# A third seven-product pair in the odd gate/up blocks, with two of its weight sums moved to idle rows

## The chip, the core and the metric

The kernel runs on one core of a Trainium2 chip, the other cores idle. The metric is the device time of one execution in microseconds (us); lower is better. Each execution is one launch that reads all weights from HBM once and writes the output. Five engines work at the same time, each through its own queue in order: PE (TensorE, the matmuls), DVE (VectorE), ACT (ScalarE), POOL (GpSimd, which only issues small DMAs in the part that matters here) and SP (SyncE, which issues the weight loads).

## The reference

One decoder layer on 256 tokens of width 2048: a gated feed-forward network, a mixer (linear attention and dilated attention side by side), and a second gated feed-forward network. The change touches the first half of the two feed-forward networks alone:

```python
D_MODEL, SEQ, D_FF = 2048, 256, 5632

def swiglu(x, w_gate, w_up, w_down):
    return (jax.nn.silu(x @ w_gate) * (x @ w_up)) @ w_down

x = x + 0.5 * swiglu(rms_norm(x, ffn1_norm), ffn1_w_gate, ffn1_w_up, ffn1_w_down)
... # mixer
x = x + 0.5 * swiglu(rms_norm(x, ffn2_norm), ffn2_w_gate, ffn2_w_up, ffn2_w_down)
```

Everything is float32. The matmuls run in a reduced form (fp32r), so each operand is cut into a high part and a low rest, and a product is made of three matmuls: high by high, high by low, low by high.

## The kernel before, in words

**Gate/up.** `x @ w_gate` and `x @ w_up` are computed together in 11 blocks of 512 columns (`FF // 512`), in each feed-forward network. A block has 16 slices of the inner dimension of 128 rows each, taken as 8 k-pairs. One load on SP's queue (L220) brings a k-pair's weights, 1 MB, into the tile `raw`, laid out [128, 2 slices, gate and up, 512]; there are three `raw` buffers. The tokens are two groups of 128, so a block's result is four PSUM banks of 128x512: two token groups times gate and up.

**A plain k-pair.** Each of its two slices is a unit. `split` cuts the 128x1024 weights of a unit: ACT copies them to the high part `wh` (L114), then DVE subtracts to get the rest `wl` (L115). `products` (L277, L279, L281) then issues 12 matmuls for the unit: two token groups, two banks, three each. A plain k-pair costs 24 matmuls, 2 copies on ACT and 2 subtractions on DVE.

**A seven.** In the blocks of `FF_SEVEN` (1 to 10) two of the eight k-pairs are computed as a 2x2 by 2x2 block product with seven block products in place of eight (Winograd's form of Strassen's method). `seven_products` issues 21 matmuls (L302 to L304). For that, `seven` prepares the weights in four parts, in this order:

- `plain`: a 128x1024 sum into `room["sum"]` (DVE, L241), and the split of two of the raw quarters;
- `last`: the split of the fourth quarter alone, 128x512, into tiles of its own (`swh`, `swl` in the profile);
- `sums`: two 128x512 additions in place in `raw` (L249, the second needs the first), and the split of `room["sum"]`;
- `more`: the split of the two quarters of `raw` that hold those additions.

The sums of activations that a seven needs (`seven_forms`, L320 to L326 and a split) are made once for each feed-forward network and used by all of its blocks. k-pairs 0 and 1 are the sevens of every block, so there are two such sets, `forms[0]` and `forms[1]`.

**The fold and the evacuation.** The seven products accumulate partly in the four banks of the result (`cs`), partly in four others (`ms`). After the last seven of a block, `fold` combines the four `ms` banks: one ACT copy (L483) and four DVE additions (L484 to L487), one for each step, into the four rows p1, u1, u2, u3 of `xs[:, 1, :]`. At the end of the block `evac` adds those rows to the banks, applies silu and the product (L451 to L454), transposes in 32x32 squares (L129), has POOL issue 16 small DMAs for each token group (L136), and a later step `finish` splits the result into `uh`, `ul`. Between a block's evacuation and the next block's fold the four rows are idle.

**The order.** `FF_ORDERS` writes the order of plain (s) and seven (g) k-pairs in a block: `ssgssgss` in blocks 1 to 10, `ssssssss` in block 0. `weights()` keeps the prepared weights up to three units ahead of the matmuls, but the order on each engine is set when the program is built, by a scheduler that estimates times; an instruction can be placed ahead of earlier lines if its inputs are ready. What limits how far DVE and ACT run ahead of PE are the buffers: four each of `wh` and `wl`, one `swh`, `swl`, one `room["sum"]`, three of `raw`. Side jobs (`later`: the `finish` steps, in block 1 also `seven_forms`) are spread over the steps of the plain units of a block, two steps a unit.

**The rest.** The down projections and the output projection have sevens too, through the same function `seven`, with `rooms["down"]`.

Of the kernel before, what the change touches and what calls it, by code (L numbers as in the profile page):

```python
# [28 lines left out]
EPS = 1e-6  # L29
WBUF = 4  # L30
FF_SEVEN = range(1, 11)
TAIL = 4
WARM = 10
GH, GDK, GDV, RANK = 4, 128, 256, 16
# [7 lines left out]
    return [(next(seven), True) if c == "g" else (next(plain), False) for c in text]  # L42


FF_ORDERS = [_order("ssgssgss" if b in FF_SEVEN else "ssssssss") for b in range(FF // 512)]
DOWN_ORDERS = [_order("ssssssgssgssgsgsgsgsss"), _order("sgsssgssgssgssgsgsssss")]
OUT_ORDERS = [_order("ssssssss"), _order("ssgsgsss")]

# [1 line left out]
def layer_kernel(tc, x, xT, gains, gla_gate_up, gla_gate_bias, gla_out_norm, att_q_norm, att_k_norm,  # L50
# [6 lines left out]
    with ExitStack() as es:  # L57
# [135 lines left out]
        def wtile(name):  # L193
            return wp.tile([P, 2, 512], F32R, name=name, tag=name, bufs=WBUF)
# [39 lines left out]
        def seven(part, w):  # L234

            raw = raws[0].bitcast(F32)
            room = rooms["gate" if w is w_ff1 or w is w_ff2 else "down"]
            if part == "plain":
                b1 = raw[:, 0, 0, :].unsqueeze(1).to_broadcast([P, 2, 512])
                mid = raw.rearrange("p k j f -> p (k j) f")[:, 1:3, :]  # L240
                nc.vector.tensor_add(room["sum"], b1, mid)  # L241
                wh, wl = wtile("wh"), wtile("wl")
                split(wh, wl, mid)
            elif part == "last":
                wh, wl = room["wh"], room["wl"]
                split(wh[:, 0, :], wl[:, 0, :], raw[:, 1, 1, :])
            elif part == "sums":
                for j, b in enumerate((room["sum"][:, 0, :], raw[:, 1, 0, :])):
                    nc.vector.tensor_add(raw[:, 1, j, :], b, raw[:, 1, j, :])  # L249
                wh, wl = wtile("wh"), wtile("wl")  # L250
                split(wh, wl, room["sum"])
            else:
                wh, wl = wtile("wh"), wtile("wl")
                split(wh, wl, raw[:, 1])
            ready.append((wh, wl))

        def weights(early=False):
# [173 lines left out]
        def ffn(name, done, residual, extra=None, final=False):  # L431

            with tc.tile_pool(name=name, bufs=1, reuse_waits="tile") as fp:

                tail = FT - TAIL
                us_h = [fp.tile([P, tail, S], F32R, name="uh")]
                us_l = [fp.tile([P, tail, S], F32R, name="ul")]
                spare = ExitStack()
                urs = xs[:, 0, 0:NT * 512].rearrange("p (t f) -> p t f", t=NT)
                extra_sums, tails = [], []  # L440

                def part(k):
                    n = int(k >= tail)
                    return us_h[n], us_l[n], k - n * tail

                for b in range(FF // 512):
                    def evac(t, ps, b=b):
                        sg, u = t512("sg"), t512("u")
                        if b in FF_SEVEN:
                            rest = extra_sums[2 * t:2 * t + 2]  # L450
                            nc.vector.tensor_sub(halves(sg), ps[0], rest[0])  # L451
                            nc.scalar.activation(sg, sg, AF.Silu, scale=rt[:, t:t + 1])
                            nc.vector.tensor_add(rest[1], ps[1], rest[1])
                            nc.vector.scalar_tensor_tensor(halves(u), rest[1], rt[:, t:t + 1], halves(sg), op0=ALU.mult, op1=ALU.mult)  # L454
                        else:
                            nc.scalar.activation(halves(sg), ps[0], AF.Silu, scale=rt[:, t:t + 1])
                            nc.vector.scalar_tensor_tensor(halves(u), ps[1], rt[:, t:t + 1], halves(sg), op0=ALU.mult, op1=ALU.mult)

                        us = t512("us")
                        ur = urs[:, t, :]  # L460
                        squares(us, u)
                        move_squares(ur, us)

                        def finish():
                            uh, ul, k = part(4 * b)
                            split(*(runs(a[:, k:k + 4, t * P:(t + 1) * P]) for a in (uh, ul)), in_order(ur))

                        put = later if 4 * b < tail else tails
                        put.extend([lambda: None] * (2 if t else 6) + [finish])
                    if b == FF_SEVEN[0]:  # L470
                        sp = spare.enter_context(tc.tile_pool(name=name + "s", bufs=1, reuse_waits="tile"))
                        t4 = xs[:, 1, :].rearrange("p (i f) -> p i f", i=4)
                        p1, u1, u2, u3 = [halves(t4[:, i, :]) for i in range(4)]
                        extra_sums = [u1, p1, u3, u2]
                        room = rooms["gate"] = {"sum": xs[:, 0, NT * 512:].rearrange("p (j f) -> p j f", j=2)}
                        for n in ("wh", "wl"):
                            room[n] = sp.tile([P, 1, 512], F32R, name="s" + n)
                        fs = [sp.tile([P, 2, 4, P], F32R, name="f" + n) for n in "hl"]
                        forms = {kp: [f[:, kp] for f in fs] for kp in range(2)}
                        later[:0] = [lambda kp=kp: seven_forms(hacts[2 * kp:2 * kp + 2], forms[kp], t4[:, 0, :], t4[:, 1, :]) for kp in range(2)]  # L480

                        def fold(m):
                            return [lambda: nc.scalar.activation(p1, m[0], AF.Copy),  # L483
                                    lambda: nc.vector.tensor_add(u1, p1, m[2]),  # L484
                                    lambda: nc.vector.tensor_add(u2, u1, m[3]),
                                    lambda: nc.vector.tensor_add(u1, u1, m[1]),
                                    lambda: nc.vector.tensor_add(u3, u2, m[1])]  # L487
                    if b in FF_SEVEN:
                        seven_pair(hacts, FF_ORDERS[b], forms, b % 2, evac, fold)
                    elif b:  # L490
                        column_pair(hacts, evac)
                    else:
                        column_pair(hacts, evac, span=16, due=8 if final else 15, extra=extra)
                spare.close()
                nc.gpsimd.dma_start(xs[:, 1, :], residual[P:2 * P, :])
                rp = spare.enter_context(tc.tile_pool(name=name + "t", bufs=1, reuse_waits="tile"))
                us_h.append(rp.tile([P, TAIL, S], F32R, name="uh2"))
                us_l.append(rp.tile([P, TAIL, S], F32R, name="ul2"))
                urs = rp.tile([P, NT, 512], F32, name="urs")
                later.extend(tails + [lambda: nc.gpsimd.dma_start(xs[:, 0, :], residual[0:P, :])])  # L500

                dacts = [part(k) for k in range(FT)]

                rooms["down"] = {"sum": urs, "wh": lent(hl, 8, 0), "wl": lent(hl, 10, 0)}
                dforms = {kp + 1: [lent(hh, 2 * kp, 1), lent(hl, 2 * kp, 1)] for kp in range(4)}
                dforms[0] = [lent(hh, 12, 1), lent(hh, 14, 1)]
                dforms[5] = [lent(hl, 12, 1), lent(hl, 14, 1)]
                rest, later[:] = later[:], []
                for step in range(32):
                    kp = step // 5 - 1  # L510
                    if step % 5 == 0 and 0 <= kp < 6:
                        later.append(lambda kp=kp: seven_forms(dacts[2 * kp:2 * kp + 2], dforms[kp], t512("full"), t512("sums")))
                    else:
                        later.append(rest.pop(0) if rest else lambda: None)
                for cp in range(2):
                    def evac(t, ps, cp=cp):
                        for j in range(2):
                            c = 2 * cp + j
                            blk = xs[:, t, c * 512:(c + 1) * 512]
                            nc.vector.scalar_tensor_tensor(halves(blk), ps[j], 0.5, halves(blk), op0=ALU.mult, op1=ALU.add)  # L520
                            done(t, c, blk)

                    def fold(m, cp=cp):
                        return fold_into_xs(m, cp, urs, 0.5)

                    holding[0] = NT - cp
                    seven_pair(dacts, DOWN_ORDERS[cp], dforms, cp, evac, fold, span=28 if cp else 32, final=final and cp == 1)
                spare.close()
# [459 lines left out]
```

## Time and profile before

| | us |
|---|---|
| median of three runs | 1718.4 |
| lowest, highest | 1717.45, 1718.85 |
| span of the profiled execution, first to last instruction | 1715.9 |
| PE busy in it | 1705.4 |
| DVE busy | 1416.9 |
| ACT busy | 947.1 |

The span leaves out what lies before the first and after the last instruction; the median of the runs stands 2.5 us above it. Lines of the profile name an engine, a line of the kernel, an operation and its tiles (`wl<-raw,wh`), how often it ran, and the idle time before it with what ended it (`[0.43 <-DMA raw]`). In a timeline the first number is the start in us from the beginning of the span, the second the duration. In the first feed-forward network, gate/up block 3 runs on PE from 130.94 us to 171.10 us, blocks 1 and 2 before it and block 4 after it in steps of the same length.

### The profile page before, as it was taken

To read this page: it belongs to the slowest core of one execution; us is meant where nothing else is said; L and a number is where in the kernel's file an instruction comes from. 1 tells how busy PE (TensorE), PEld (TensorE's weight loads), DVE (VectorE), ACT (ScalarE), POOL (GpSimd) and SP (SyncE) were. 2 spreads that over 40 slices of the span, in tenths; PEclk is the share of its full clock that TensorE was granted. 3 is DMA by queue.
4 is the path that set the end of the run, shared out by engine and by line. 5 is a ranking of instruction groups with operands and counts; after the bars stand their busy time and mean duration, and the time that the engine had idled before them with its cause. 6 is when DMAs were issued, how large, how long until landed. Compare 5 with 4: busy or idle time off the path is not lost.

```text
span 1715.9 us, 22309 instructions
## 1 busy us (share of the span) xinstructions
PE 1705.4 (99%) x7974; PEld 1485.1 (87%) x7974; DVE 1416.9 (83%) x1731; ACT 947.1 (55%) x1173; POOL 505.7 (29%) x1002
## 2 busy tenths in 40 slices
PE   9999999999999999999999999999999999999999
PEld 7888888888888888888888888888888888888887
DVE  6888889898898788577865788788888898898876
ACT  7555555555555555564654555555555555555453
POOL 0333334344410611054250043333333333420000
PEclk9999999999999999999999999999999999999999
DMA  8666666556665657577564467666666666665654
GB/s 345 213 229 224 219 211 232 208 213 236 234 250 219 217 203 244 192 237 235 195 210 172 148 198 269 210 231 225 222 224 220 226 212 224 218 242 222 248 204 147
DMA packets 85807, 378.62 MB, mean 221 GB/s; under 512 B 21392, under 2 KB 38800, under 8 KB 42688
## 3 DMA queue, kind: packets, MB, share of 16 engines
q1 hardware_dynamic: 50864, 350.25, 57.2%
q0 software_dynamic: 34112, 25.88, 5.3%
q8 instruction: 62, 1.02, 0.2%
q10 hardware_dynamic: 720, 1.07, 0.2%
q14 instruction: 49, 0.40, 0.1%
HBM read 354.57 MB, written 4.19 MB: 209 GB/s over the span
## 4 chain that ended last, share of the span: by engine, by line
PE 89%; DMA 4%; DVE 4%; POOL 1%; issue 1%; ACT 0%; DVEq 0%; SPq 0%; ACTq 0%; POOLq 0%
PE acc L279 20%; PE acc L277 20%; PE acc L281 20%; PE tp L281 4%; PE tp L277 4%; PE tp L279 4%; PE acc L303 4%; PE acc L304 4%; PE acc L302 4%; DVE wl L115 2%; DMA raw<-in_w_dn_dram 2%; DMA hh<-us 1%; PE tp L303 1%; PE tp L304 1%; PE tp L302 1%
## 5 line engine op out<-in xcount | busy, mean ns | idle before, releaser
L114 ACT ACTIVATE wh<-raw 128x1024 fp32r<-128x1024 f32 (+1 forms) x660 | 683.6, 1048 | 531.2 <-PE acc L281 186.6
L115 DVE TENSOR_TENSOR wl<-raw,wh 128x1024 fp32r<-128x1024 f32 (+1 forms) x658 | 790.3, 1215 | 168.4 <-ACT wh L114 165.0
L136 POOL DMA_DIRECT2D xs<-us x704 | 344.9, 497 | 552.1 <-ACT wh L114 200.3
L281 PE MATMUL acc<-wh,hl 128*128 128x512 f32 x1232 | 370.7, 380 | 0.0
L279 PE MATMUL acc<-wl,hh 128*128 128x512 f32 x1232 | 369.9, 380 | 0.1
L277 PE MATMUL acc<-wh,hh 128*128 128x512 f32 x1232 | 363.5, 381 | 2.6 <-ACT wh L114 2.6
L277 PEld LDWEIGHTS acc<-wh,hh 128*128 128x128 f32 x1232 | 232.3, 189 | 37.7 <-ACT wh L114 4.1
L279 PEld LDWEIGHTS acc<-wl,hh 128*128 128x128 f32 x1232 | 232.6, 189 | 33.9 <-issue 0.7
L281 PEld LDWEIGHTS acc<-wh,hl 128*128 128x128 f32 x1232 | 232.6, 189 | 32.9 <-DVE hl L544 0.2
L279 PE MATMUL acc<-wl,uh 128*128 128x512 f32 x384 | 117.2, 380 | 0.0
L281 PE MATMUL acc<-wh,ul 128*128 128x512 f32 x384 | 117.0, 379 | 0.0
L277 PE MATMUL acc<-wh,uh 128*128 128x512 f32 x384 | 112.1, 380 | 0.7 <-ACT wh L114 0.7
L136 POOL DMA_DIRECT2D hh<-us x128 | 62.4, 506 | 126.7 <-DVE us L129 69.0
L241 DVE TENSOR_TENSOR xs<-raw 128x1024 f32<-128x1024 f32 x40 | 49.0, 1225 | 46.9 <-DMA raw<-in_w_ff_dram 46.9
L277 PEld LDWEIGHTS acc<-wh,uh 128*128 128x128 f32 x384 | 72.3, 189 | 12.0 <-ACT wh L114 1.9
L279 PEld LDWEIGHTS acc<-wl,uh 128*128 128x128 f32 x384 | 72.4, 189 | 10.8 <-DVE wl L115 0.6
L281 PEld LDWEIGHTS acc<-wh,ul 128*128 128x128 f32 x384 | 72.6, 189 | 10.3
L277 PE MATMUL tp<-wh,hh 128*128 128x512 f32 x240 | 73.2, 379 | 0.0
L281 PE MATMUL tp<-wh,hl 128*128 128x512 f32 x240 | 71.4, 379 | 0.0
L279 PE MATMUL tp<-wl,hh 128*128 128x512 f32 x240 | 71.4, 379 | 0.0
L114 ACT ACTIVATE wh<-xs 128x1024 fp32r<-128x1024 f32 x40 | 42.2, 1055 | 45.2 <-PE acc L281 24.1
L114 ACT ACTIVATE swh<-raw 128x512 fp32r<-128x512 f32 x40 | 25.3, 631 | 60.6 <-DMA raw<-in_w_ff_dram 60.6
(326 smaller groups left out, 2382.3 us busy)
## 6 DMA issues: line engine op xcount, KB each, us to landing
raw<-in_w_ff_dram SPq DMA_DIRECT2D x175, 1024.0 KB, 5.0
raw<-in_w_dn_dram SPq DMA_DIRECT2D x88, 1024.0 KB, 4.9
raw<-in_w_mix_dram SPq DMA_DIRECT2D x48, 1024.0 KB, 5.0
raw<-in_w_out_dram SPq DMA_DIRECT2D x16, 1024.0 KB, 4.8
xs<-us POOLq DMA_DIRECT2D x704, 16.0 KB, 3.4
xs<-in_x_dram SPq DMA_DIRECT2D x2, 1024.0 KB, 9.8
xs<-in_x_dram POOLq DMA_DIRECT2D x2, 1024.0 KB, 5.4
hh<-us POOLq DMA_DIRECT2D x128, 16.0 KB, 3.7
```

The costliest lines, as they stand in the source:

```text
L114: nc.scalar.activation(dst_h, src, AF.Copy)
L115: nc.vector.tensor_sub(dst_l, src, dst_h.bitcast(F32))
L136: nc.gpsimd.dma_start(dst[32 * q:32 * q + 32, ..., r * n:(r + 1) * n], src[32 * r:32 * r + 32, ..., q * n:(q + 1) * n])
L241: nc.vector.tensor_add(room["sum"], b1, mid)
L277: nc.tensor.matmul(ps[j], lhsT=sh, rhs=alt(wh[:, j, :]), start=first and i == 0, stop=False)
L279: nc.tensor.matmul(ps[j], lhsT=sh, rhs=alt(wl[:, j, :]), start=False, stop=False)
L281: nc.tensor.matmul(ps[j], lhsT=sl, rhs=alt(wh[:, j, :]), start=False, stop=last and i == len(ws) - 1)
L302: nc.tensor.matmul(bank, lhsT=a[0], rhs=alt(ws[0][:, j, :]), start=start, stop=False)
L303: nc.tensor.matmul(bank, lhsT=a[0], rhs=alt(ws[1][:, j, :]), start=False, stop=False)
L304: nc.tensor.matmul(bank, lhsT=a[1], rhs=alt(ws[0][:, j, :]), start=False, stop=stop)
```

## The change

In the blocks 1, 3, 5, 7 and 9 a third k-pair is a seven, and the order there becomes `ssgsggss`: the second and third seven follow each other. The even blocks keep two. The third set of activation sums, `forms[2]`, lies in two rows of `us_h` and `us_l` that block 9 fills at its end.

The two additions that stood in part `sums` (L249) are made in part `plain`, right after the first sum, and write the idle fold rows p1 and u1 (`room["more"]`) in place of `raw`; the split of part `more` reads them there. So `raw` is last read in part `last`. This holds for all sevens of the gate/up blocks, even ones too; the sevens of the down and output projections keep the old form. `seven_forms` uses the other two rows as scratch. The last two additions of the fold become one instruction over 128x1024 elements.

```diff
+FF_THREE = range(1, 10, 2)
...
-FF_ORDERS = [_order("ssgssgss" if b in FF_SEVEN else "ssssssss") for b in range(FF // 512)]
+FF_ORDERS = [_order("ssgsggss" if b in FF_THREE else "ssgssgss" if b in FF_SEVEN else "ssssssss") for b in range(FF // 512)]
...
                 nc.vector.tensor_add(room["sum"], b1, mid)
+                if "more" in room:
+                    for j, b in enumerate((room["sum"][:, 0, :], room["more"][:, 0, :])):
+                        nc.vector.tensor_add(room["more"][:, j, :], b, raw[:, 1, j, :])
                 wh, wl = wtile("wh"), wtile("wl")
                 split(wh, wl, mid)
...
             elif part == "sums":
-                for j, b in enumerate((room["sum"][:, 0, :], raw[:, 1, 0, :])):
-                    nc.vector.tensor_add(raw[:, 1, j, :], b, raw[:, 1, j, :])
+                if "more" not in room:
+                    for j, b in enumerate((room["sum"][:, 0, :], raw[:, 1, 0, :])):
+                        nc.vector.tensor_add(raw[:, 1, j, :], b, raw[:, 1, j, :])
                 wh, wl = wtile("wh"), wtile("wl")
                 split(wh, wl, room["sum"])
             else:
                 wh, wl = wtile("wh"), wtile("wl")
-                split(wh, wl, raw[:, 1])
+                split(wh, wl, room["more"] if "more" in room else raw[:, 1])
...
-                        room = rooms["gate"] = {"sum": xs[:, 0, NT * 512:].rearrange("p (j f) -> p j f", j=2)}
+                        room = rooms["gate"] = {"sum": xs[:, 0, NT * 512:].rearrange("p (j f) -> p j f", j=2), "more": t4[:, 0:2, :]}
...
-                        later[:0] = [lambda kp=kp: seven_forms(hacts[2 * kp:2 * kp + 2], forms[kp], t4[:, 0, :], t4[:, 1, :]) for kp in range(2)]
+                        forms[2] = [lent(a[0], 36, 1) for a in (us_h, us_l)]
+                        later[:0] = [lambda kp=kp: seven_forms(hacts[2 * kp:2 * kp + 2], forms[kp], t4[:, 2, :], t4[:, 3, :]) for kp in range(3)]
...
-                                    lambda: nc.vector.tensor_add(u1, u1, m[1]),
-                                    lambda: nc.vector.tensor_add(u3, u2, m[1])]
+                                    lambda: nc.vector.tensor_add(v4(t4[:, 1::2, :]), v4(t4[:, 1:3, :]),
+                                                                 m[1].unsqueeze(1).to_broadcast([P, 2, 2, 256]))]
```

More of the change, by code (lines that the diff above doesn't have):

```diff
@@ L473, in ffn @@
                         p1, u1, u2, u3 = [halves(t4[:, i, :]) for i in range(4)]
+                        v4 = lambda a: a.rearrange("p i (b a) -> p i b a", b=2)
                         extra_sums = [u1, p1, u3, u2]
-                        room = rooms["gate"] = {"sum": xs[:, 0, NT * 512:].rearrange("p (j f) -> p j f", j=2)}
+                        room = rooms["gate"] = {"sum": xs[:, 0, NT * 512:].rearrange("p (j f) -> p j f", j=2), "more": t4[:, 0:2, :]}
                         for n in ("wh", "wl"):
```

## The prediction

> **What bounds the kernel now.** I read the page first, then the clock and the table of stages, then the timelines of PE, DVE and ACT in two blocks of gate/up, last the waits.
>
> ```profile
> span 1715.9 us, 22309 instructions
> PE 1705.4 (99%) x7974; PEld 1485.1 (87%) x7974; DVE 1416.9 (83%) x1731; ACT 947.1 (55%) x1173; POOL 505.7 (29%) x1002
> PEclk9999999999999999999999999999999999999999
> PE 89%; DMA 4%; DVE 4%; POOL 1%; issue 1%; ACT 0%; DVEq 0%; SPq 0%; ACTq 0%; POOLq 0%
> ```
>
> PE is busy throughout at the full clock, and 89% of the chain that ends last is PE. A matmul less is therefore time less, as long as no other engine becomes the later one. The next engine is DVE. The table of stages, one row for each of the blocks 1, 3 and 4:
>
> ```profile
> 50.62:90.79 40.17, 40.17 (x187) 35.16 (x187) 33.20 (x37) 22.08 (x24) 15.76 (x32) 1.00 0.64 223
> 130.94:171.10 40.16, 40.16 (x188) 35.16 (x187) 35.80 (x41) 23.03 (x26) 15.66 (x32) 1.00 0.63 223
> 171.10:211.26 40.16, 40.16 (x188) 35.17 (x187) 35.81 (x41) 22.21 (x24) 15.68 (x32) 1.00 0.64 222
> ```
>
> After the length stand PE, PE's loads, DVE, ACT, POOL, the clock, the DMA share and GB/s. PE has no gap in these blocks; DVE works 35.8 of 40.16 us. Averaged over the kernel DVE looks harmless at 83%; in the stage that the change edits it has 4.4 us to spare in a block.
>
> **What PE saves.** PE's timeline around the second seven of block 2 and the plain units behind it:
>
> ```profile
> 116.05 0.38 PE L302 MATMUL acc<-wh,hh 128*128 128x512 f32 x1
> ...
> 120.58 1.03 PE L277 MATMUL acc<-wh,hh 128*128 128x512 f32 x4
> ...
> 123.17 1.03 PE L277 MATMUL acc<-wh,hh 128*128 128x512 f32 x4
> ```
>
> The seven takes 120.58 - 116.05 = 4.53 us for 21 matmuls, a plain unit 2.59 us for 12, so a plain k-pair 5.18 and a matmul 0.216. A pair that turns into a seven saves 0.65 us. Five blocks in two networks: 10 x 0.65 = 6.5 us. An odd block on PE becomes 40.16 - 0.65 = 39.5 us.
>
> **What DVE pays.** The groups by shape, and DVE's timeline from the end of block 2 into block 3:
>
> ```profile
> L115 DVE TENSOR_TENSOR wl<-raw,wh 128x1024 fp32r<-128x1024 f32 x654 | 787.6, 1218 | 163.3 <-ACT wh L114 159.9
> L114 ACT ACTIVATE wh<-raw 128x1024 fp32r<-128x1024 f32 x654 | 680.5, 1053 | 522.8 <-PE acc L281 186.6 <-DVE raw L249 148.6 <-PE tp L281 87.9
> L241 DVE TENSOR_TENSOR xs<-raw 128x1024 f32<-128x1024 f32 x40 | 49.0, 1225 | 46.9 <-DMA raw<-in_w_ff_dram 46.9
> L249 DVE TENSOR_TENSOR raw<-raw 128x512 f32<-128x512 f32 x66 | 45.3, 687 | 1.2
> L487 DVE TENSOR_TENSOR xs<-xs,acc 128x512 f32<-128x512 f32 x20 | 13.6, 678 | 0.0
> ```
>
> ```profile
> 127.05 1.22 DVE L115 TENSOR_TENSOR wl<-raw,wh 128x1024 fp32r<-128x1024 f32 x1 [0.81 <-ACT wh L114]
> 128.71 1.22 DVE L241 TENSOR_TENSOR xs<-raw 128x1024 f32<-128x1024 f32 x1 [0.43 <-DMA raw<-in_w_ff_dram]
> 129.85 0.68 DVE L115 TENSOR_TENSOR swl<-raw,swh 128x512 fp32r<-128x512 f32 x1
> 130.45 0.68 DVE L451 TENSOR_TENSOR sg<-acc,xs 128x512 f32<-128x512 f32 x1
> ...
> 139.24 0.68 DVE L249 TENSOR_TENSOR raw<-xs,raw 128x512 f32<-128x512 f32 x1
> 139.85 0.74 DVE L454 SCALAR_TENSOR_TENSOR u<-xs,rt,sg 128x512 f32<-128x512 f32 x1
> 140.51 0.68 DVE L249 TENSOR_TENSOR raw<-raw 128x512 f32<-128x512 f32 x1
> 141.11 0.70 DVE L129 STREAM_TRANSPOSE us<-u 128x512 f32<-128x512 f32 x1
> 142.39 4.71 DVE L115 TENSOR_TENSOR wl<-raw,wh 128x1024 fp32r<-128x1024 f32 x4 [0.58 <-ACT wh L114]
> 148.72 1.23 DVE L241 TENSOR_TENSOR xs<-raw 128x1024 f32<-128x1024 f32 x1 [1.61 <-DMA raw<-in_w_ff_dram]
> 149.86 1.22 DVE L115 TENSOR_TENSOR wl<-raw,wh 128x1024 fp32r<-128x1024 f32 x1
> ```
>
> I cost by start to start, not by duration: the 1024-wide sum at 128.71 is followed after 1.14 us, the 512-wide split at 129.85 after 0.60, though they are shown as 1.22 and 0.68 long. A plain k-pair on DVE is 2 x 1.14 = 2.28. A seven is a sum and three splits, 4 x 1.14, plus the small split 0.60 and two additions, 1.3 together with the short wait of the second for the first: 6.46. So a third seven adds 4.2 us to DVE in an odd block. The merged fold addition replaces two of 0.60 by one of at most 1.22 (the row of L115, not so wide a reach for an operand in PSUM; L487 shows that a PSUM operand costs 678 ns at 512 where L249 has 687); I take 1.14, a gain of 0.06. Odd block: 35.8 + 4.2 - 0.1 = 39.9 us of DVE against 39.5 of PE. The even block behind it keeps 35.8 against 40.16, so over two blocks DVE needs 75.7 of 79.7 us. On average it fits; inside the odd block it doesn't by 0.4 us, and what DVE is ahead has to carry it.
>
> VectorE: DVE Perf Modes of the Trainium skill, section The TRN2 errata, gives a two-input fp32 addition (N+151)/0.96 ns, so 1224 and 691, and calls the fixed part exposed between instructions. The durations here (1225 and 687) agree, the 1.14 start to start does not; what the rule would give stands among the rivals.
>
> **Does what DVE is ahead suffice?** The hard place is the pair of sevens in a row: PE takes 2 x 4.53 = 9.06 us for them, DVE 2 x 6.46 = 12.9. Counted from the start of block 3 on PE, 130.94, with DVE's order as it stands: it finishes the first seven and three plain units by 142.39 + 4.71 = 147.1, so the first seven and two plain units at about 145.9, which is 15.0 us into the block. In the changed odd block the second seven is next: 15.0 + 6.46 = 21.5. Then of the third the sum and, now ahead of the split, the two additions, 2.44, and the first split 1.14: 25.0. PE comes to the third seven at 4 x 2.59 + 4.53 + 5.18 + 4.53 = 24.6 and wants the rest `wl` one matmul later, 24.8. So with nothing better than before PE would wait 0.2 us in each odd block.
>
> Two things make it better. First, DVE's 0.58 us of idle time at 142.39 should go. PE and ACT show why it is there:
>
> ```profile
> 141.30 2.96 ACT L114 ACTIVATE wh<-raw 128x1024 fp32r<-128x1024 f32 x3 [3.25 <-DVE raw L249]
> ```
>
> ```profile
> 144.54 0.38 PE L302 MATMUL acc<-wh,fh 128*128 128x512 f32 x1
> 144.76 0.38 PE L302 MATMUL tp<-wh,hh 128*128 128x512 f32 x1
> 144.97 0.59 PE L277 MATMUL acc<-wh,hh 128*128 128x512 f32 x2
> 145.41 0.38 PE L277 MATMUL tp<-wh,hh 128*128 128x512 f32 x1
> 145.62 0.38 PE L303 MATMUL acc<-wl,fh 128*128 128x512 f32 x1
> ```
>
> ACT's copy for part `more` waited for the late additions, with the next units' copies behind it in its queue, and DVE then waited for ACT (148.6 us of such ACT waits in all, row L114). With the additions made early this order is gone: 0.4 us to spare instead of 0.2 late. Second, PE bends: at 144.54 its order takes the high parts of three products first and the rest `wl` 1.1 us after the `wh` of the same tile. If the same is done at the third seven, up to about 0.65 us (three matmuls) of lateness cost nothing.
>
> The raw buffers loosen too:
>
> ```profile
> SPq L220 <- DVE wl L115: 1415.7, 303, 10.7
> ```
>
> The loads wait for the last split that reads a buffer. In block 3 that is the split at 142.39, about 143.5 when done, and the next seven's sum, three k-pairs on and so in the same buffer, starts 5.2 us later at 148.72 after 1.61 us of idle time. Now the buffer is free after the small split, some three to four us earlier, and most of that 46.9 us of L241 waits (1.2 for a seven) should go. Block 3's sum at 128.71 follows a plain pair, not a seven; its 0.43 stays.
>
> **The small parts.** The third set of activation sums is made once for each network; block 0's timeline shows one of the present two:
>
> ```profile
> 37.55 0.75 DVE L320 TENSOR_TENSOR xs<-hh,hl 128x256 f32<-128x256 f32 x2
> ...
> 40.07 0.68 DVE L115 TENSOR_TENSOR fl<-xs,fh 128x512 fp32r<-128x512 f32 x1
> ```
>
> From 37.55 to the end of that split are 3.2 us with other work between, so at most that of DVE in block 0 or 1, where block 1 has 40.17 - 33.20 = 7.0 us free before its third seven takes 4.2. Hidden; uncovered it would cost at most 3.2 us twice. ACT gets two copies more and a small one, some 1.6 us on 23: hidden. DMA moves as many bytes, and POOL's small DMAs stay as many; the `finish` steps come in 20 steps a block instead of 24, behind the two sevens in the written order. If one (0.60 of DVE) slips in ahead of them, the 0.4 to spare becomes 0.2 late, inside PE's 0.65. At a block's first seven the additions move ahead of the first split and must wait for the last reader of row p1 in the evacuation, on the same engine; that split then ends 1.3 us later than the 138.2 of before or less, where PE wants it at 141.3: hidden.
>
> **The sum.** With 0.4 us to spare and the bending behind it most odd blocks should lose nothing; for single late splits I put 0.1 us in each. Against the profiled execution: 1715.9 - 6.5 + 10 x 0.1 = 1710.4; the median of the runs lies 2.5 above the span, so 1712.9.
>
> **The rivals.** *DVE a little late.* If the idle time at the first seven stays and a `finish` slips in, or if DVE waits for the raw buffer once before the pair of sevens, PE comes late by 0.2 + 0.6 = 0.8, or by 1.61 - 0.4 = 1.2, less what it bends, up to 0.65: some 0.3 to 1.0 us in each odd block, 1715 to 1722. For it: 39.9 of 39.5 us leaves no room inside the block. Against: the orders that made the idle time are what the change removes. DVE's instructions could also follow each other at their full duration, 1.22 and 0.69: the 10.0 us from 15.0 to 25.0 become (4 x 1.22 + 3 x 0.69) + (2 x 1.22 + 2 x 0.69) = 10.8, so PE waits 0.4 to 1.0 us ten times, the same times; the starts at 128.71 and 129.85 speak against it, so 0.04 of this case's chance. (That is what the rule of the Trainium skill above makes of the change.)
>
> *Slower: DVE stands behind a raw load in front of the pair of sevens.* Place: the sum of the second or third seven. DVE's order is fixed, and at 148.72 it waited 1.61 us for a load with a split queued behind whose copy was long there:
>
> ```profile
> 146.68 1.06 ACT L114 ACTIVATE wh<-raw 128x1024 fp32r<-128x1024 f32 x1 [0.84 <-PE tp L304]
> ```
>
> That copy was done at 147.74 and its split ran only at 149.86. (TensorE: Matmul & The Clock Gate in the Trainium skill, section Architectural detail, says the same: ACT and DVE are strict FIFO.) If both sums wait so, 1.2 us each, less the 0.4 to spare and as much of PE's bending, PE loses 1.6 us ten times: 1718.4 - 6.5 + 16 = 1728. It decides from 1.0 us of lost PE time in an odd block, 6.5 + 3.4 over ten. Against: the third seven's buffer is that of the first seven, free by some 10 us into the block and loaded by 15; the second's is that of a plain pair, free at about 4.
>
> *The clock or another stage eats it.* A down stage in the same trace shows PE waits that come back in other places when the order shifts:
>
> ```profile
> 500.00:560.00 60.00, 58.69 (x270) 50.42 (x269) 53.10 (x57) 33.60 (x37) 0.00 (x0) 1.00 0.61 226
> ```
>
> 1.3 us lost in 60, with DVE at 53.1 and alternating sevens: this is what too little room looks like, and at 1.00 the clock did not fall. At worst that again in both networks, within the range.
>
> **The numbers.** About 0.2%, 3.4 us, is what a measurement of this kernel can tell from no change. The forecast (under 0.3 us lost in an odd block, so below 1715) gets 0.60; a little late, between 1715 and 1721.8, 0.24; slower, 0.16. The range: at the bottom no wait at all and the scatter of the runs, 1711.0; at the top most of the second case, 1720.5.
>
> **What would show it.** Right: PE's stage row for an odd block 39.5 us long with PE gapless, DVE at 39 to 40 in it; 30 matmuls fewer; no ACT copy that waits for the additions; the waits of L241 for the load far below 46.9 although there are 50 of them. Wrong: waits of PE for `wl` at the third seven of an odd block, DVE idle behind a load in front of it, or odd blocks over 40.5 us.

## The result and the profile after

| | before | after |
|---|---|---|
| median of five runs, us | 1718.4 | 1712.9 |
| lowest to highest | 1717.1 to 1720.6 | 1710.0 to 1713.1 |
| span of the profiled execution | 1715.9 | 1711.2 |
| PE matmuls | 7974 | 7944 |

The ratio is 0.9964, with a 95% interval from 0.9952 to 0.9976: a gain of 0.36%, clear of the 0.2% that a measurement of this kernel can tell. First the page of after:

```profile
span 1711.2 us, 22342 instructions
PE 1701.1 (99%) x7944; PEld 1480.4 (87%) x7944; DVE 1451.1 (85%) x1775; ACT 964.8 (56%) x1195; POOL 506.4 (30%) x1002
```

PE has 30 matmuls fewer and 4.3 us less busy time, DVE 34 us more. The table of stages, for block 3 of the first network, which PE begins at 131.73 in this execution, and then from the first seven of block 1 to that of block 10, in the first network and in the second:

```profile
131.73:171.23 39.50, 39.50 (x184) 34.59 (x183) 37.76 (x43) 24.56 (x28) 15.67 (x32) 1.00 0.65 227
63.75:422.05 358.30, 358.30 (x1661) 313.47 (x1660) 334.23 (x375) 210.25 (x235) 139.75 (x286) 1.00 0.63 222
1099.31:1457.38 358.07, 358.07 (x1661) 313.55 (x1659) 335.18 (x374) 209.68 (x234) 139.10 (x286) 1.00 0.64 223
```

The odd block is 39.5 us long, and PE has no gap in it or in either of the long stretches. DVE's timeline in block 3, around the third seven (PE runs the matmuls of its part `last` from 156.8):

```profile
152.40 1.23 DVE L242 TENSOR_TENSOR xs<-raw 128x1024 f32<-128x1024 f32 x1
153.67 0.69 DVE L245 TENSOR_TENSOR xs<-xs,raw 128x512 f32<-128x512 f32 x1
154.28 1.22 DVE L116 TENSOR_TENSOR wl<-raw,wh 128x1024 fp32r<-128x1024 f32 x1
155.41 0.69 DVE L245 TENSOR_TENSOR xs<-xs,raw 128x512 f32<-128x512 f32 x1
156.01 0.69 DVE L116 TENSOR_TENSOR swl<-raw,swh 128x512 fp32r<-128x512 f32 x1
156.62 1.22 DVE L116 TENSOR_TENSOR wl<-xs,wh 128x1024 fp32r<-128x1024 f32 x1
...
166.35 2.36 DVE L116 TENSOR_TENSOR wl<-raw,wh 128x1024 fp32r<-128x1024 f32 x2
170.42 1.23 DVE L242 TENSOR_TENSOR xs<-raw 128x1024 f32<-128x1024 f32 x1 [1.70 <-DMA raw<-in_w_ff_dram]
```

From block 3's own first sum, at 129.67, no row has idle time before it until the next block's first sum at 170.42: DVE runs without a pause for 39.0 us, to 168.7, and then waits 1.70 us for a load. The second addition of the third seven (155.41) stands ahead of the small split (156.01) and of the split of the first sum (156.62); the second of these turns out to matter. ACT's copies for the last part of block 3's first seven and of its third:

```profile
140.47 1.06 ACT L115 ACTIVATE wh<-xs 128x1024 fp32r<-128x1024 f32 x1 [1.34 <-DVE xs L245]
...
156.21 1.06 ACT L115 ACTIVATE wh<-xs 128x1024 fp32r<-128x1024 f32 x1 [0.20 <-DVE xs L245]
```

The third seven's copy waits 0.20 us for that addition. The first seven's waits 1.34; before, the same copy had waited 3.25 (at 141.30). Two groups of after:

```profile
L242 DVE TENSOR_TENSOR xs<-raw 128x1024 f32<-128x1024 f32 x50 | 61.3, 1225 | 29.7 <-DMA raw<-in_w_ff_dram 29.7
L493 DVE TENSOR_TENSOR xs<-xs,acc 128x1024 f32<-128x1024 f32 x20 | 24.4, 1219 | 0.0
```

The first sums wait 29.7 us for their loads, 0.6 a seven where it was 1.2, and the merged fold addition with an operand in PSUM takes 1219 ns, as a 1024-wide one in SBUF does.

### The profile page after: what moved, and what is told of

Same layout as the page of the kernel before. It is cut to its first block, busy times and chain, and to the rows that moved or that the text cites. A ratio compares the mean times of both kernels' runs of the same rounds, so it can differ in the third digit from the quotient of the medians.

```text
span 1711.2 us, 22342 instructions
## 1 busy us (share of the span) xinstructions
PE 1701.1 (99%) x7944; PEld 1480.4 (87%) x7944; DVE 1451.1 (85%) x1775; ACT 964.8 (56%) x1195; POOL 506.4 (30%) x1002
## 4 chain that ended last, share of the span: by engine, by line
PE 92%; DMA 3%; DVE 3%; POOL 2%; issue 1%; ACT 0%; SPq 0%; DVEq 0%; ACTq 0%; POOLq 0%
PE acc L284 20%; PE acc L286 20%; PE acc L282 20%; PE acc L308 5%; PE acc L309 5%; PE acc L307 5%; PE tp L286 4%; PE tp L284 4%; PE tp L282 4%; DVE wl L116 1%; PE tp L309 1%; PE tp L308 1%; PE tp L307 1%; DMA hh<-us 1%; POOL hh L137 1%
## 5 line engine op out<-in xcount | busy, mean ns | idle before, releaser
L115 ACT ACTIVATE wh<-raw 128x1024 fp32r<-128x1024 f32 (+2 forms) x610 | 631.1, 1048 | 443.5 <-PE acc L286 194.2
L116 DVE TENSOR_TENSOR wl<-raw,wh 128x1024 fp32r<-128x1024 f32 (+1 forms) x608 | 732.2, 1218 | 147.9 <-ACT wh L115 145.3
L284 PE MATMUL acc<-wl,hh 128*128 128x512 f32 x1192 | 358.9, 381 | 0.1
L282 PE MATMUL acc<-wh,hh 128*128 128x512 f32 x1192 | 349.0, 381 | 2.2 <-ACT wh L115 1.9
L115 ACT ACTIVATE wh<-xs 128x1024 fp32r<-128x1024 f32 x100 | 105.6, 1056 | 104.1 <-DVE xs L245 33.1
L116 DVE TENSOR_TENSOR wl<-xs,wh 128x1024 fp32r<-128x1024 f32 x100 | 120.8, 1218 | 2.4 <-ACT wh L115 2.4
L242 DVE TENSOR_TENSOR xs<-raw 128x1024 f32<-128x1024 f32 x50 | 61.3, 1225 | 29.7 <-DMA raw<-in_w_ff_dram 29.7
L286 PEld LDWEIGHTS acc<-wh,ul 128*128 128x128 f32 x384 | 72.6, 189 | 10.3
L245 DVE TENSOR_TENSOR xs<-xs,raw 128x512 f32<-128x512 f32 x100 | 68.7, 687 | 0.4
L282 PE MATMUL tp<-wh,hh 128*128 128x512 f32 x200 | 61.6, 379 | 0.0
L286 PE MATMUL tp<-wh,hl 128*128 128x512 f32 x200 | 59.5, 379 | 0.0
```

The lines of the kernel that those rows point to most:

```text
L115: nc.scalar.activation(dst_h, src, AF.Copy)
L116: nc.vector.tensor_sub(dst_l, src, dst_h.bitcast(F32))
L245: nc.vector.tensor_add(room["more"][:, j, :], b, raw[:, 1, j, :])
L282: nc.tensor.matmul(ps[j], lhsT=sh, rhs=alt(wh[:, j, :]), start=first and i == 0, stop=False)
L284: nc.tensor.matmul(ps[j], lhsT=sh, rhs=alt(wl[:, j, :]), start=False, stop=False)
L286: nc.tensor.matmul(ps[j], lhsT=sl, rhs=alt(wh[:, j, :]), start=False, stop=last and i == len(ws) - 1)
```

## The experiments

Twelve kernels, all timed in five rounds against the kernel before on the same chip.

**The additions alone** (`FF_THREE = range(0)`, two sets of activation sums).

> Two sevens in every block as before, with the early additions in the idle rows and the merged fold. Theory (the gain is the 30 matmuls that PE no longer runs; the early additions only make room on DVE): no matmul is saved and PE had no gap in gate/up, so 1718.4 within 1.5 us, while the waits of the first sum for its load fall from 46.9 us to under 25 and ACT's waits for the additions, in gate/up, go. Rival (the early additions themselves bring time): 1716 or less.

Measured: 1719.1, ratio 1.0004 (0.9995 to 1.0013). PE has no gap between the first sevens of blocks 1 and 10 and no matmul less, and nothing is gained.

```profile
L242 DVE TENSOR_TENSOR xs<-raw 128x1024 f32<-128x1024 f32 x40 | 49.0, 1225 | 28.6 <-DMA raw<-in_w_ff_dram 28.6
```

The sum's waits fell from 46.9 to 28.6 us and bought no time: they had been covered. They didn't fall under 25, and ACT's waits for the additions didn't go: 34.7 us are left. The place of the additions is no gain in itself.

**The third seven alone** (the additions stay in the raw tile).

```diff
-room = rooms["gate"] = {"sum": ..., "more": t4[:, 0:2, :]}
+room = rooms["gate"] = {"sum": ...}
```

> Three sevens in the odd blocks, but the two additions stay late and in place in the raw tile, as before the change. Theory (without the early additions DVE comes 0.2 us late at the third seven, and the raw buffer of the first seven is held some 4 us longer): PE loses 0.2 to 1.0 us in each odd block, 2 to 10 us on 1711.9, so 1714 to 1722, likeliest 1716. Rival (the place of the additions doesn't matter, what DVE is ahead covers it): 1712.9 within 1.5, as the changed kernel.

Measured: 1719.6, ratio 1.001 (1.0001 to 1.0019). The same 30 matmuls are gone and the time is not less. The third seven of block 3, on DVE, ACT and PE:

```profile
153.76 1.22 DVE L116 TENSOR_TENSOR wl<-xs,wh 128x1024 fp32r<-128x1024 f32 x1
154.89 0.68 DVE L254 TENSOR_TENSOR raw<-xs,raw 128x512 f32<-128x512 f32 x1
155.50 0.69 DVE L116 TENSOR_TENSOR ul<-xs,uh 128x512 fp32r<-128x512 f32 x1
156.10 0.68 DVE L116 TENSOR_TENSOR swl<-raw,swh 128x512 fp32r<-128x512 f32 x1
156.82 0.69 DVE L254 TENSOR_TENSOR raw<-raw 128x512 f32<-128x512 f32 x1
158.69 3.50 DVE L116 TENSOR_TENSOR wl<-raw,wh 128x1024 fp32r<-128x1024 f32 x3 [1.18 <-ACT wh L115]
```

```profile
157.60 4.93 ACT L115 ACTIVATE wh<-raw 128x1024 fp32r<-128x1024 f32 x5 [0.89 <-DVE raw L254]
```

```profile
158.71 0.48 PE L307 MATMUL acc<-wh,uh 128*128 128x512 f32 x1 [0.47 <-ACT wh L115]
159.66 0.70 PE L282 MATMUL acc<-wh,hh 128*128 128x512 f32 x2 [0.25 <-ACT wh L115]
```

The second addition overwrites the quarter that the small split `swl` reads, so it must follow it; here both additions also stand behind the split of the first sum (153.76). ACT's copy follows the addition; DVE idles 1.18 us for the copy; PE waits. From block 3's first seven to block 5's, two blocks, PE takes 80.9 us in place of 79.6 after the change. From block 1's first seven to block 10's it takes 362.2 us in the first network and 362.9 in the second, where after has 358.3 and 358.1: 8.7 us for ten odd blocks, 0.9 in each, more than the 0.65 that each saves.

**Late in the text, but in the idle rows.** The same two additions, moved back into part `sums`, still writing `room["more"]`.

> The changed kernel, the two additions still written to the idle rows but made late, in part sums, where they stood before. This keeps the rows and gives up the early time: the raw tile is again read by the additions, a little earlier freed than by the last split. With late additions in the raw tile PE lost 0.9 to 1.6 us in an odd block and the time was 1719.6. Theory (the time of the additions counts, since ACT's copy of the last part waits for them with the next copies behind it): 1716 to 1720, with ACT's waits for the additions above 100 us. Rival (the place counts, since it frees the raw tile): 1712.9 within 1.5.

Measured: 1712.4, ratio 0.9965 (0.9952 to 0.9977). My theory was that the earlier line counts; it falls. The scheduler puts the additions early anyway:

```profile
156.10 0.69 DVE L251 TENSOR_TENSOR xs<-xs,raw 128x512 f32<-128x512 f32 x1
156.70 0.69 DVE L116 TENSOR_TENSOR swl<-raw,swh 128x512 fp32r<-128x512 f32 x1
157.30 1.22 DVE L116 TENSOR_TENSOR wl<-xs,wh 128x1024 fp32r<-128x1024 f32 x1
```

This is the order of after: the second addition ahead of both splits. What frees it is the row it writes, not the line it stands in.

**In the rows, but tied behind the splits.** That leaves two things which the row changes: the order, and how long the raw tile is held. This kernel keeps the row and forces late additions with two one-column copies.

```diff
+nc.vector.tensor_copy(room["more"][:, j, 0:1], w[:, 0, 0:1].bitcast(F32))  # w: wl of plain, then of last
 nc.vector.tensor_add(room["more"][:, j, :], b, raw[:, 1, j, :])
```

> The additions write the idle rows, but two DVE copies of one column (0.1 us each) make the first addition wait for the split of part plain and the second for the split of part last, which is the order that additions in place in the raw tile are bound to, since those splits read the quarters that they overwrite. The raw tile is still freed by the second addition, before the split of part more. Theory A (the order counts: late additions hold ACT's copy of the last part): 1717 to 1721, near the 1719.6 of late additions in the raw tile. Theory B (the earlier release of the raw tile counts): 1713 to 1715.

Measured: 1728.3, ratio 1.0066 (1.0052 to 1.008). Beyond my range on the side of theory A. The same place in block 3:

```profile
158.32 1.06 ACT L115 ACTIVATE wh<-xs 128x1024 fp32r<-128x1024 f32 x1 [3.37 <-DVE xs L253]
```

```profile
L242 DVE TENSOR_TENSOR xs<-raw 128x1024 f32<-128x1024 f32 x50 | 61.1, 1222 | 16.4 <-DMA raw<-in_w_ff_dram 16.4
```

ACT's copy waits 3.37 us for the addition, and so does all behind it in ACT's queue. Loads aren't the cause: the first sums wait 16.4 us for them, less than the 29.7 of after. So late additions alone take more than the gain. But the order that this kernel forces isn't quite the old one: ACT's copies wait 139 us for the additions in gate/up, where the third seven alone has some 110 (174.6 in all, less the 65 that after shows for the sevens with additions in the raw tile). The loss of 15 us against after also contains the one-column copies' own DVE time, about 0.1 us each; the split of the loss wasn't measured.

**The raw tile held, and its control.** A DVE instruction of one column in part `more`, in all sevens, reads the raw tile; in the control it reads the idle row.

```diff
+nc.vector.tensor_add(junk[:, 0:1], wl[:, 1, 511:512].bitcast(F32), raw[:, 1, 1, 511:512])
+# control: ... room["more"][:, 1, 511:512] in place of raw
```

> The changed kernel with one more DVE instruction of one column in part more, which reads the raw tile after the last split, so that the raw tile is held as long as before the change; the additions stay early. The instruction itself is about 0.15 us, 0.45 in an odd block. Theory (early additions keep ACT's copies moving, the raw tile's earlier release is the lesser part): 1712.9 to 1715. Rival (the release of the raw tile is what made room for the third seven): 1716 to 1720, with waits of the first sum for its load back above 40 us.

> Control to the kernel that held the raw tile (1722.9): the same DVE instruction of one column in part more, but reading the idle row instead of the raw tile, so nothing is held. Theory B, or both theories at work (holding the raw tile costs by itself): 1713 to 1717, at least 5 us under 1722.9. Rival (the instruction on a full DVE made the 10 us): 1720 or more.

Measured: 1722.9, ratio 1.0023 (1.0012 to 1.0033), against 1711.1, 0.9964 (0.9951 to 0.9976), for the control. The instruction costs nothing that the runs can tell, the held tile 12 us by the medians and 10 by the ratios. First the kernel that holds it, then the control:

```profile
L115 ACT ACTIVATE wh<-raw 128x1024 fp32r<-128x1024 f32 x604 | 623.8, 1052 | 439.8 <-PE acc L288 155.9 <-DMA raw<-in_w_ff_dram 89.6 <-PE tp L288 69.9
L242 DVE TENSOR_TENSOR xs<-raw 128x1024 f32<-128x1024 f32 x50 | 61.1, 1222 | 42.1 <-DMA raw<-in_w_ff_dram 42.0
```

```profile
L242 DVE TENSOR_TENSOR xs<-raw 128x1024 f32<-128x1024 f32 x50 | 61.1, 1223 | 27.7 <-DMA raw<-in_w_ff_dram 27.6
```

Loads come late: ACT's copies wait 89.6 us for them, where the control's row doesn't name the load among its three largest. The additions come later too: ACT's copies for the last part wait 84.8 us for them, in the control 41.4, so not every microsecond is the load's own. So the row does two things, and either one undone, in these kernels, takes the whole gain. The two losses don't add up: with both undone (the third seven alone) it is 7 to 8 us, and the builder makes another order of each kernel.

**How much DVE has to spare.** Additions of 128x512 (0.6 us each) into a scratch tile, in part `plain` of the third seven of each odd block: one, two, four. And four in the second seven of each even block.

```diff
+if rooms["i"] % 8 == 2:
+    for _ in range(n):
+        nc.vector.tensor_add(junk, raw[:, 1, 0, :], raw[:, 1, 1, :])
```

> One 128x512 addition more (0.6 us) on DVE in the third seven of each odd block. Two cost 15 us and four 31, so a line through them and through no cost at no addition gives 7.7 us. If DVE's way to the third seven has nothing to spare: 1719 to 1722. If 0.4 us or more is to spare, as the prediction had it, and two merely overran it: 1713 to 1716.

> The changed kernel with two 128x512 additions more on DVE, into a scratch tile, in part plain of the third seven of each odd block: 1.2 us. Theory (in the changed kernel DVE runs without a gap through an odd block but for about 1.7 us at its end, and PE bends by 0.65 us or more): the 0.4 us to spare and the bending take most of it, 0 to 0.4 us lost in each odd block, 1712.5 to 1717. Rival (DVE has much more room, since the buffers hold it back): 1712.9 and no wait, at this dose and at twice it.

> As the kernel with two additions more, with four: 2.4 us. Theory: 2.4 less the 0.4 to spare and the bending of 0.65 leaves 1.0 to 1.4 us lost in each odd block, 1722 to 1728, with PE waiting for wh or wl at or after the third seven. Rival (DVE has much more room): 1712.9 and no wait.

> Four 128x512 additions more (2.4 us) on DVE in the second seven of each even block with sevens, none in the odd blocks. Theory (DVE has some 4 us to spare in an even block, and the odd block starts with what the buffers hold): 1713 to 1716. Rival (DVE lags everywhere by now and any added work is paid in full): 1730 or more.

| added on DVE, a block | us | ratio to before |
|---|---|---|
| odd, 0.6 us | 1712.1 | 0.9970 (0.9960 to 0.9981) |
| odd, 1.2 us | 1728.3 | 1.0061 (1.0049 to 1.0073) |
| odd, 2.4 us | 1743.8 | 1.0148 (1.0135 to 1.0161) |
| even, 2.4 us | 1714.8 | 0.9982 (0.9973 to 0.9991) |

0.6 us can't be told from free (its profile has 0.6 us of PE waits in the whole of gate/up), 1.2 us is not free; the even blocks take 2.4 us each for 2 to 3 us of the whole time. But two and four cost more than I expected, 15 and 31 us over ten odd blocks. With two, ACT and PE in block 3:

```profile
157.66 1.06 ACT L115 ACTIVATE wh<-xs 128x1024 fp32r<-128x1024 f32 x1 [2.50 <-DVE xs L246]
```

```profile
158.77 0.48 PE L311 MATMUL acc<-wh,uh 128*128 128x512 f32 x1 [0.44 <-ACT wh L115]
...
159.72 0.70 PE L286 MATMUL acc<-wh,hh 128*128 128x512 f32 x2 [0.25 <-ACT wh L115]
```

Once late, PE takes each high part as it comes and then waits for the next copy too: these two places make up 1.2 of the 1.3 us that are lost between block 3's first seven and block 5's. But the added work isn't all that differs. The second addition of the third seven in block 3 and the split of the first sum, with one and then with two additions more:

```profile
154.91 0.68 DVE L246 TENSOR_TENSOR xs<-xs,raw 128x512 f32<-128x512 f32 x1
155.51 1.22 DVE L116 TENSOR_TENSOR wl<-xs,wh 128x1024 fp32r<-128x1024 f32 x1
```

```profile
155.72 1.23 DVE L116 TENSOR_TENSOR wl<-xs,wh 128x1024 fp32r<-128x1024 f32 x1
156.85 0.69 DVE L246 TENSOR_TENSOR xs<-xs,raw 128x512 f32<-128x512 f32 x1
```

With two, the builder has put the second addition behind the split of the first sum, and ACT's copy waits 1.13 us more for that. In the other order the addition would start at 155.72 and end at 156.41; the copy, 1.06 us long, would be done by about 157.5, ahead of the 158.2 at which PE wants it. By this estimate 1.2 us would have been free too, and the step between 0.6 and 1.2 is that of the builder's order; no run has two additions in the old order. The small split doesn't matter: with one addition more, and in the control above, the second addition stands behind it in block 3 and nothing is lost there.

**Three sevens in each of the blocks 1 to 9.**

> Three sevens in each of the blocks 1 to 9, early additions as changed: eight more sevens in all. PE saves another 8 x 0.65 = 5.2 us, 1707.7 if nothing is lost. Theory (DVE needs 39.9 us for the 39.5 of such a block, and the even block with two sevens is what gives it back): the loss begins once what DVE is ahead is used up, 0.4 to 1.0 us a block in most of 18 blocks, so 1711 to 1720, with waits of PE for wh and wl in gate/up. Rival (DVE is further from its bound than the rows say): 1707 to 1709, no waits.

Measured: 1726.3, ratio 1.0052 (1.0038 to 1.0066), later than I put it. The first sevens of blocks 1, 2, 3 and 5 on PE, and a wait in block 3:

```profile
61.85 0.38 PE L307 MATMUL acc<-swh,hh 128*128 128x512 f32 x1
...
101.35 0.38 PE L307 MATMUL acc<-swh,hh 128*128 128x512 f32 x1
...
140.84 0.38 PE L307 MATMUL acc<-swh,hh 128*128 128x512 f32 x1
...
158.12 0.48 PE L307 MATMUL acc<-wh,uh 128*128 128x512 f32 x1 [0.54 <-ACT wh L115]
...
223.74 0.38 PE L307 MATMUL acc<-swh,hh 128*128 128x512 f32 x1
```

Blocks 1 and 2 take 39.5 us each, without loss; from block 3 to 5 two blocks take 82.9 in place of 79.0. Against 39.5 a block the two networks lose 10.3 and 9.0 us up to block 10's first seven, 1.1 a block over all 18 blocks, just above the 0.4 to 1.0 that I gave, and 1.4 from block 3 on. It fits the theory, that what DVE is ahead is used up in two such blocks. The order changes there as well: in block 2 the second addition of the third seven stands ahead of the split of the first sum, in block 3 behind it. In the second network that order begins in block 4, and the loss too: 39.8 us for block 3, 41.3 for block 4. The runs don't separate what DVE lacks from what the order costs.

**The sevens taken apart** (`ssgsgsgs` in the odd blocks). With one plain pair behind the last seven the evacuation of the first token group reads row u1 one step before its last addition, so this kernel leaves that term out; the work is the same in another order.

> The changed kernel with the order ssgsgsgs in the odd blocks: no two sevens follow each other, and one plain pair instead of two is left behind the last one for the fold. Theory (the pair of sevens in a row is covered in the changed kernel, PE has no gap there): no gain from taking it apart, 1712.9 within 1.5 us, or later if the fold then crowds the next block's evacuation. Rival (the two in a row cost time that is hidden in the sum): 1711 or less.

Measured: 1712.1, ratio 0.9965 (0.9953 to 0.9978). As after: two sevens in a row cost nothing that taking them apart would save.

## Why the prediction was right, and where it wasn't

**What PE saves** was right to a hundredth for a block. From block 1's first seven to block 2's PE took 40.14 us before and 39.50 after, 0.64 for the predicted 0.65. Up to block 10's, five odd blocks, the first network saves 3.2 us (361.5 to 358.3). The second saves 4.1, since before has a loss of 0.84 us in one block there, part of it as a gap of PE (361.84 busy of 362.14), which after doesn't have:

```profile
1100.02:1462.16 362.14, 361.84 (x1675) 316.22 (x1674) 321.15 (x360) 202.74 (x226) 137.19 (x281) 1.00 0.64 222
```

**The wait term**, 10 x 0.1, was mis-sized: it is nothing, as the stage rows of both networks show. **The 2.5 us outside the span** were mis-sized too: the profiled execution of after took 1713.0 by its own time, 1.8 above its span, and the other executions listed stand about as far above theirs; the remaining 0.7 is then a difference between the executions of before. And a term was missing. PE's block 1 began later in this execution; its first seven's small matmul, before and after:

```profile
62.31 0.38 PE L302 MATMUL acc<-swh,hh 128*128 128x512 f32 x1
```

```profile
63.75 0.38 PE L307 MATMUL acc<-swh,hh 128*128 128x512 f32 x1
```

1.44 us, from the clock at the start (below). What lies between the two stretches took 1.1 us more, what follows them 0.1; why stays open. So 1715.9 - 3.2 - 4.1 + 1.4 + 1.2 = 1711.2, and 1.8 on top gives 1713.0. That the forecast of 1712.9 met the median is in part luck: it had 1.0 us of waits that didn't come and 0.7 too much outside the span, and saw 0.8 too little saved; against these stand 1.4 us of clock and 1.2 elsewhere that it didn't have.

**DVE's load.** The forecast was 39.9 us of DVE in an odd block for 39.5 of PE, too much by 0.4. The row of PE's block 3 shows 37.8. That row cuts DVE's work elsewhere than the row of before did; counted on DVE itself, from block 3's first sum to block 4's, it is 39.0 busy in 40.75 us. So DVE fits with some 0.5 us, and does wait at the end. The step that was off is the 35.8 of before: counted start to start, as the seven was, the work of such a block comes to some 35 (an estimate from the rows), and the 4.1 added to it were about right.

**DVE's margin.** 0.4 us to spare and 0.65 of bending made 1.05 us. The kernels lose nothing at 0.6 and lose at 1.2, which fits; but the loss at 1.2 came with another order, so the margin itself isn't confirmed.

**Why there is room** was right in effect and wrong in its agent. I wrote that the additions are made early and that ACT is then no longer held. The late line in the idle rows did as well as the early one; the row counts, because it overwrites nothing that the two splits still read, and so lets the builder put the additions ahead of the split of the first sum. In the odd blocks from 5 on, in both networks, every kernel that keeps the gain or most of it has both additions of the third seven ahead of that split. Every kernel that loses it has the second one or both behind it, except the one that holds the raw tile, which has both ahead and waits for loads. That is a pattern over twelve kernels; no run changes this order alone. One sign that I had named didn't come: ACT's copies still wait for the additions, 33.1 us in after's gate/up. These waits cost nothing, since PE has no gap. And the earlier release of the raw tile, which I took for a loosening beside it, is as necessary: holding it cost 10 to 12 us.

**The rivals.** None came as written. *A little late* is what the third seven does without the rows (1719.6). The other reading there, that instructions follow each other at their full duration, would have PE wait in each odd block, and it doesn't wait in after, nor does 0.6 us more cost what can be told. The *slower* one, DVE behind a load, comes close to what the held raw tile does (1722.9), though there ACT's copies wait for the loads as well as DVE's sums. Of the third, the clock did take its part, 1.4 us at the start. My price for overrunning the margin was too small: 1.2 us against about 1.05 should cost 0.15 us a block and cost 1.5, most of it, by the estimate above, through the order.

## What to carry to other kernels

When an engine beside the bound one has a few per cent left in a stage, ask of each intermediate what it overwrites: an in-place sum is chained to every reader of the old value and keeps its buffer from the next load. Here the row that it wrote counted, and the line that it stood in didn't. Find the margin by adding known work until time moves; the average share of busy time tells little, since here 0.6 us in a 39.5 us block cost nothing that could be told and 1.2 us cost more than it took. Then compare the order of instructions with and without the added work: where a scheduler sets it, the order may be what moved. A saving on the bound engine is worth its full price only if no gap opens there, so look for gaps at the place where two dear steps follow each other.

## What the runs showed of the hardware

The clock at the start isn't the same in each of the profiles. In the seven us from 13 on, before and then after:

```profile
13.00:20.00 7.00, 5.98 (x26) 4.94 (x27) 6.07 (x8) 6.26 (x9) 0.00 (x0) 1.00 1.03 412
```

```profile
13.00:20.00 7.00, 6.22 (x20) 4.87 (x21) 6.33 (x9) 6.20 (x9) 0.00 (x0) 0.76 1.03 414
```

PE's timeline of after there:

```profile
13.64 1.13 PE L282 MATMUL acc<-wh,hh 128*128 128x512 f32 x4 [1.69 <-ACT wh L115]
14.91 1.06 PE L284 MATMUL acc<-wl,hh 128*128 128x512 f32 x2
```

Behind a gap of 1.69 us matmuls follow each other at 0.43 us instead of 0.216 until 18.3, and 6 fewer run in the seven us. Before has a gap of 1.72 us at the same place and no drop. Of the fourteen profiles of this case, each of another kernel, three show it, behind gaps of 1.69, 2.17 and 2.26 us; eleven, with gaps from 0.82 to 1.72, don't. TensorE: Matmul & The Clock Gate of the Trainium skill, in its part on the clock gate, has the clock halve after an idle window of about 3.4 us and return after as long a busy one. The 3.4 us at half clock agree; the gap here is half of what the Trainium skill gives, so the length of one gap alone doesn't decide it.
